# Output projection by token group, with row sums beside its last group, early operands for the second feed-forward product, and its context rows last

## The chip, the cores and the metric

The kernel runs on one core of a Trainium2 chip. TensorE (PE) multiplies matrices and accumulates in PSUM; VectorE (DVE), ScalarE (ACT) and GpSimd (POOL) work elementwise; SyncE (SP) issues DMA transfers, and so do ACT and POOL, each from a queue of its own that it works off in order. The metric is the device time of one execution in microseconds (us), the median over several runs.

## The reference

One layer of a hybrid backbone is applied to 1024 latent and 256 context tokens of width 1024. The part that the change touches begins after the three branches have been merged:

```python
x = x + gt1 * (merged @ w_out)
u2 = rmsnorm(x, g_norm2) * (1 + sc2) + sh2
x = x + gt2 * (jnp.square(jax.nn.relu(u2 @ w_ff1)) @ w_ff2)
...
y_prompt = rmsnorm(xc, g_final)
y_sample = rmsnorm(xs, g_final)
```

`w_out` is 1024 x 1024, `w_ff1` 1024 x 4096, `w_ff2` 4096 x 1024. Latent and context tokens use the same weights and different modulation vectors. Before this part stand an input norm, the combined input projection, and the pooling, gating and mLSTM branches; the change leaves them alone.

## The kernel before

**Precision.** Every large product runs on float32 operands split into a high part `hi` (rounded to float32r, an ACT cast) and a rest `lo` (a DVE subtraction), and takes three matmuls: hi by hi, hi by lo, lo by hi. So each operand that a product needs costs one ACT and one DVE instruction first.

**Tokens.** There are ten tiles of 128 tokens in three groups: 0 (tiles 0 to 3), 1 (tiles 4 to 7) and 2 (tiles 8 and 9, the context). The buffer `z` holds ten rows of 1024 floats; `xt[i]` is row i, and `zs(j)` is the j-th half row, so `xt[i]` is `zs(2i)` and `zs(2i+1)`.

**Output projection (lines 847 to 867).** The outer loop runs over four quarters q of 256 output columns. Each quarter loads two halves of `w_out` (`load_w`, lines 90 to 96: a 512 KB transfer, an ACT cast, a DVE subtraction), then goes over all ten tiles with 24 matmuls each. DVE multiplies the result by the gate and adds it to `xt`, ACT squares it for the norm. In the last quarter each tile is stored to `scr_x`, and after tiles 3, 7 and 9 `modulate_ff(g)` (lines 807 to 845) turns a finished group into the operands of the feed-forward part: a row scale whose power POOL computes (line 131), scaled rows `xn`, PE transposes (line 831), an ACT evacuation with scale and bias (lines 835 and 840), and splits on DVE (lines 836, 837, 843, 844). `load_w` has two raw and three hi and lo slots (pool `wp`), the small temporaries five (pool `tp`).

**First product (lines 876 to 1030).** Latent tokens use a 2 x 2 block scheme with seven products instead of eight: blocks B11, B21, B12, B22 of the activations (row halves by token groups 0 and 1) and four combinations T1 to T4 of them, made by 16 DVE subtractions (line 879) and split at lines 880 to 887. The 4096 hidden columns are 16 pairs fp. A `Pair` loads its two weight rows to `z`; `begin` computes the products with B11 and B21 and, between them, the four context products (`context`, lines 936 to 942); `rest` computes the other five (T4, T2, T3, T1, B22); `sums` stores the squared results to `scr_h`, `scr_c` and their combinations to `scr_s` and `scr_c`, all from ACT's queue (lines 995 to 1006). `second_sums` loads `w_ff2` rows to `zs(8..11)`, combines them on POOL (line 1015) and stores them to `scr_t`. Pool `q1`, which holds the split operands (`ring`, nine tiles, tag w), the temporaries (tag s, six) and six tiles of tag th, lies over the memory of `tp` and `wp`; it opens after the projection.

**Second product (lines 1042 to 1149).** Seven passes i = 1, 2, 6, 7, 4, 5, 3 go over the 16 pairs. `operand` loads and splits a right block (512 columns of `w_ff2` or of `scr_t`), a left block (512 columns of `scr_h` or `scr_s`, four token tiles) and a context block (128 columns of `scr_c`); 15 matmuls per pair follow, into five PSUM banks, of eight. The last pass goes twice over the pairs, with three banks and then two. `evict` combines the passes with two accumulators U and W, gates and adds them to `xt`, and `finish_rows` does the final norm and stores `y_out`. The rows `xt` are read back from `scr_x` by ten POOL transfers ahead of the passes (line 1043).

**Order.** In this part nothing is pinned: a list scheduler orders the instructions of each engine at build time, by program order as priority and by a simulated timeline.

Of the kernel before, what the change touches and what calls it, by code (L numbers as in the profile page):

```python
# [14 lines left out]
P = 128  # L15
# [34 lines left out]
def hybrid_step(  # L50
# [14 lines left out]
    sp = pa.enter_context(tc.tile_pool(name="sp", bufs=60))  # L65
    tp = pw.enter_context(tc.tile_pool(name="tp", bufs=NTMP))
    wp = pw.enter_context(tc.tile_pool(name="wp", bufs=NRAW))
# [779 lines left out]
    for q in range(4):  # L847
        wq = [load_w(w_out[q, hf], f"wo{q}_{hf}") for hf in range(2)]
        for i in range(NT):
            g, o = (i * P) // 512, (i * P) % 512  # L850
            ps = ps_mm(f"po{q}_{i}")
            for k in range(KT):
                whi, wlo = wq[k // 4]
                s = slice((k % 4) * 256, (k % 4 + 1) * 256)
                mh, ml = mT[k][g]
                PE.matmul(ps[:, :256], mh[:, o : o + P], whi[:, s], start=k == 0, stop=False)  # L856
                PE.matmul(ps[:, :256], ml[:, o : o + P], whi[:, s], start=False, stop=False)
                PE.matmul(ps[:, :256], mh[:, o : o + P], wlo[:, s], start=False, stop=k == KT - 1)  # L858
            gt = gt1[(2 if g == 2 else 0) + q // 2][:, (q % 2) * 256 : (q % 2) * 256 + 256]
            V.tensor_tensor(ps[:, :256], ps[:, :256], gt, ALU.mult)  # L860
            xq = xt[i][:, q * 256 : (q + 1) * 256]
            V.tensor_tensor(xq, xq, ps[:, :256], ALU.add)  # L862
            A.activation(ps[:, 256:512], xq, AF.Square, accum_out=fsq[:, i, q : q + 1])  # L863
            if q == 3:
                SP.dma_start(scr_x[i], xt[i])
            if q == 3 and i in (3, 7, 9):
                modulate_ff(g)
# [8 lines left out]
    for kk in range(4):  # L876
        b11, b21, b12, b22 = raw2[0][kk], raw2[0][kk + 4], raw2[1][kk], raw2[1][kk + 4]
        for out, x, y in ((b11, b12, b11), (b12, b22, b12), (b22, b22, b11), (b21, b22, b21)):
            V.tensor_tensor(out, x, y, ALU.subtract)
        for nm, t in (("T1", b11), ("T2", b22), ("T3", b12), ("T4", b21)):  # L880
            if nm == "T4" and kk != 2:
                hi, lo = (q1.tile([P, 512], F32R, tag="th", name=f"t4{i}{kk}", bufs=6) for i in "hl")
            else:
                hi, lo = slot(f"{nm}h{kk}"), slot(f"{nm}l{kk}")
            A.copy(hi, t)
            V.tensor_tensor(lo, t, hi.bitcast(F32), ALU.subtract)
            u2s[nm, kk] = hi, lo

    NFP = NFF // 2
    scr_h = [dp.tile([P, 4, 512], F32, name=f"scr_h{fp}") for fp in range(NFP)]  # L890
    scr_c = [dp.tile([2, P, 4, P], F32, name=f"scr_c{fp}") for fp in range(NFP)]
# [24 lines left out]
    class Pair:  # L916
        def __init__(self, fp):
            self.fp = fp
            self.a1, self.a2, self.b1, self.b2 = (zs(12 + 4 * (fp % 2) + i) for i in range(4))
# [24 lines left out]
        def begin(self):  # L944
            fp = self.fp
            a11, a12, a21, a22 = self.raw
            self.pc = ps_mm(f"fc{fp}")
            w = split(a11, f"a11_{fp}")
            ps = self.prod(w, "B11")
            A.copy(self.a1, ps)  # L950
            A.copy(self.a2, ps)
            self.context(0, w, 0, True)
            w = split(a12, f"a12_{fp}")
            ps = self.prod(w, "B21")
            V.tensor_tensor(self.a1, self.a1, ps, ALU.add)  # L955
            self.squared_relu(self.a1)
            self.context(0, w, 1, False)
# [31 lines left out]
        def sums(self):  # L989
# [8 lines left out]
            A.dma_start(scr_c[fp][0], self.hc.rearrange("p (q c) -> p q c", c=P))  # L998
# [5 lines left out]
            A.dma_start(scr_c[fp][1], sc.rearrange("p (q c) -> p q c", c=P))  # L1004
            for i, t in enumerate((x1, x2, a2_, x4)):
                A.dma_start(scr_s[fp][:, i, :], t)

    def second_sums(fp):

        q = [zs(8 + i) for i in range(4)]  # L1010
        for r in range(2):
            SP.dma_start(zs(8 + 2 * r, 2), w_ff2[2 * fp + r])
        b11, b12, b21, b22 = q
        for out, x, y in ((b11, b12, b11), (b12, b22, b12), (b22, b22, b11), (b21, b22, b21)):
            G.tensor_tensor(out, x, y, ALU.subtract)  # L1015
        G.dma_start(scr_t[fp], zs(8, 4).rearrange("p (q c) -> p q c", c=512))

    pairs = {}
    for fp in (0, 1):
        pairs[fp] = Pair(fp)  # L1020
    for fp in (0, 1):
        pairs[fp].begin()
    for fp in range(NFP):
        pr = pairs.pop(fp, None)
        if pr is None:
            pr = Pair(fp)
            pr.begin()
        pr.rest()
# [13 lines left out]
    for i in range(NT):  # L1042
        G.dma_start(xt[i], scr_x[i])  # L1043
# [18 lines left out]
    def operand(src, w, tag, name, early=False):  # L1062

        def room(nm, tg, dt, bufs):
            if early or tg == "l":
                return ring(nm, dt)[:, :w]
            return q2.tile([P, P if w == P else 512], dt, tag=tg, name=nm, bufs=bufs)[:, :w]

        raw = room(f"{name}r", f"{tag}r" if w == P else "raw", F32, 4)
        SP.dma_start(raw, src)  # L1070
        hi, lo = (room(f"{name}{i}", tag if tag == "l" else f"{tag}{i}", F32R, NFP if tag == "r" else 3) for i in "hl")
        A.copy(hi, raw)  # L1072
        V.tensor_tensor(lo, raw, hi.bitcast(F32), ALU.subtract)  # L1073
        return hi, lo

# [6 lines left out]
    def finish_rows(tok, final):  # L1082
        x = xt[tok]
        sq = small([P, 2], f"sq_y{tok}")
        for hf in (0, 1):
            A.activation(tmp2(f"junk_y{tok}{hf}"), x[:, hf * 512 : hf * 512 + 512], AF.Square, accum_out=sq[:, hf : hf + 1])
        s1 = small([P, 1], f"s1_y{tok}")
        V.tensor_tensor(s1, sq[:, 0:1], sq[:, 1:2], ALU.add)  # L1088
        r = rstd_of(s1, 1, f"f{tok}")
        for hf in range(2):  # L1090
            s = slice(hf * 512, hf * 512 + 512)
            V.scalar_tensor_tensor(x[:, s], x[:, s], r[:, 0:1], gf[hf], ALU.mult, ALU.mult)
            if final:
                SP.dma_start(y_out[tok][:, s], x[:, s])
        if not final:
            SP.dma_start(y_out[tok], x)

    def evict(i, j, ps):
# [3 lines left out]
        elif i == 2:  # L1102
            t = tmp2(f"c11_{j}")
            V.tensor_tensor(t, U, ps, ALU.add)
            gated_add(t, R1[j], 0)
        elif i == 6:
# [3 lines left out]
        elif i == 4:  # L1110
            t = tmp2(f"c21_{j}")
            V.tensor_tensor(t, W, ps, ALU.subtract)
            gated_add(t, R2[j], 0)
        elif i == 5:
# [3 lines left out]
            finish_rows(R2[j], False)  # L1118
        else:
            V.tensor_tensor(U, U, ps, ALU.add)  # L1120
            gated_add(U, R1[j], 1)
            finish_rows(R1[j], j == 4)

    for n_, i in enumerate((1, 2, 6, 7, 4, 5, 3)):
        scr, at, part, cols_ = PRODUCTS[i]
        rt = [None] * NFP
        for js in ((0, 1, 2), (3, 4)) if i == 3 else ((0, 1, 2, 3, 4),):
            banks = {j: p2.tile([P, 512], F32, tag="b", name=f"w{i}_{j}", bufs=8) for j in js}
            lc = None
            for fp in range(NFP):  # L1130
                early = n_ == 0 and fp < 2
                nm = f"{i}_{fp}"
                if rt[fp] is None:
                    src = scr_t[fp][:, cols_, :] if isinstance(cols_, int) else w_ff2[2 * fp + cols_[0], :, cols_[1] * 512 : cols_[1] * 512 + 512]
                    rt[fp] = operand(src, 512, "r", f"r{nm}", early)
                rh, rl = rt[fp]
                full = [j for j in js if j < 4]
                c0, c1 = full[0] * P, full[-1] * P + P
                lh, ll = operand(scr[fp][:, at, c0:c1], c1 - c0, "l", f"l{nm}_{c0}", early)
                pieces = [(j, lh[:, j * P - c0 : j * P - c0 + P], ll[:, j * P - c0 : j * P - c0 + P]) for j in full]  # L1140
                if 4 in js:
                    ch, cl = operand(scr_c[fp][part, :, at, :], P, "lc", f"lc{nm}")
                    pieces.append((4, ch, cl))
                for j, h_, l_ in pieces:
                    PE.matmul(banks[j], h_, rh, start=fp == 0, stop=False)  # L1145
                    PE.matmul(banks[j], l_, rh, start=False, stop=False)  # L1146
                    PE.matmul(banks[j], h_, rl, start=False, stop=fp == NFP - 1)  # L1147
            for j in js:
                evict(i, j, banks[j])

# [101 lines left out]
```

## Time and profile before

| | us |
|---|---|
| median of 3 runs | 2044.52 (2043.96 to 2046.18) |
| the profiled execution | 2038.69 |
| its span, first to last instruction | 2036.9 |

The profile shows one execution, and all durations below are its own; it is 5.8 us faster than the median of the runs. Its 40 slices of 51 us say, in tenths, how busy each engine was, and what clock TensorE was granted:

```profile
PE   6999999998999999999999969999999989999996
DVE  7684444449544344444444389776766555655676
ACT  6534455653111111111132265554555444434443
POOL 3000001027012122122200034334200100000000
PEclk9999999999999999999999979999999999999999
```

Counted from 0, the output projection runs in slices 21 to 23, the first feed-forward product up to slice 31, and the second one from there to the end. A group row of the profile reads: line, engine, operation, output<-inputs, shapes, count | busy us in all, mean ns of one | idle us of the engine before them, and who ended it. In the timeline the first two columns are start and duration.

### The profile page before, as it was taken

To read this page: it belongs to the slowest core of one execution; us is meant where nothing else is said; L and a number is where in the kernel's file an instruction comes from. 1 tells how busy PE (TensorE), PEld (TensorE's weight loads), DVE (VectorE), ACT (ScalarE), POOL (GpSimd) and SP (SyncE) were. 2 spreads that over 40 slices of the span, in tenths; PEclk is the share of its full clock that TensorE was granted. 3 is DMA by queue.
4 is the path that set the end of the run, shared out by engine and by line. 5 is a ranking of instruction groups with operands and counts; after the bars stand their busy time and mean duration, and the time that the engine had idled before them with its cause. 6 is when DMAs were issued, how large, how long until landed. Compare 5 with 4: busy or idle time off the path is not lost.

```text
span 2036.9 us, 28713 instructions
## 1 busy us (share of the span) xinstructions
PE 1952.8 (96%) x10688; PEld 1681.1 (83%) x10688; DVE 1168.6 (57%) x2076; ACT 776.4 (38%) x1694; POOL 322.5 (16%) x282
## 2 busy tenths in 40 slices
PE   6999999998999999999999969999999989999996
PEld 3788889996888888888889958888888878888875
DVE  7684444449544344444444389776766555655676
ACT  6534455653111111111132265554555444434443
POOL 3000001027012122122200034334200100000000
PEclk9999999999999999999999979999999999999999
DMA  8011111113222252252232146777643576555554
GB/s 322 21 34 48 51 54 42 51 58 129 94 73 83 73 184 65 63 186 73 83 99 99 44 174 230 269 265 269 232 140 135 184 257 184 176 174 174 171 170 145
DMA packets 133100, 273.93 MB, mean 134 GB/s; under 512 B 15456, under 2 KB 39904, under 8 KB 130912
## 3 DMA queue, kind: packets, MB, share of 16 engines
q1 hardware_dynamic: 97696, 193.36, 29.5%
q10 hardware_dynamic: 28224, 48.78, 6.4%
q0 software_dynamic: 7040, 29.96, 4.0%
q8 instruction: 84, 1.38, 0.3%
q14 instruction: 56, 0.46, 0.1%
HBM read 195.98 MB, written 76.06 MB: 134 GB/s over the span
## 4 chain that ended last, share of the span: by engine, by line
PE 88%; DVE 5%; DMA 3%; issue 2%; ACT 1%; POOL 1%; SPq 0%; ACTq 0%; DVEq 0%; POOLq 0%
PE w L1145 6%; PE w L1146 6%; PE w L1147 6%; PE br L124 5%; PE br L125 5%; PE br L126 5%; PE pb L759 3%; PE pb L760 3%; PE pb L761 3%; PE fT L913 3%; PE fT L912 3%; PE fT L914 3%; PE fB L914 2%; PE fB L912 2%; PE fB L913 2%; PE po L856 2%
## 5 line engine op out<-in xcount | busy, mean ns | idle before, releaser
L754 ACT ACTIVATE sg<-br 128x512 f32<-128x512 f32 (+1 forms) x72 | 37.9, 526 | 309.9 <-PE br L126 296.9
L1015 POOL TENSOR_TENSOR z<-z 128x512 f32<-128x512 f32 x64 | 97.2, 1519 | 145.3 <-DMA z<-in_w_ff 142.2
L1073 DVE TENSOR_TENSOR l_0l<-l_0r,l_0h 128x512 fp32r<-128x512 f32 (+1 forms) x112 | 75.0, 670 | 77.1 <-PE w L1146 65.5
L446 POOL PARTITION_ALL_REDUCE acc<-acc x16 | 54.2, 3431 | 327.7 <-DVE acc L439 293.9
L439 DVE SCALAR_TENSOR_TENSOR acc<-wb,scond,acc 128x512 f32<-128x512 f32 x112 | 82.3, 792 | 14.6 <-DMA wb<-in_w_ada 14.6
L768 DVE TENSOR_TENSOR sg<-pb,sg 128x512 f32<-128x512 f32 (+1 forms) x48 | 28.8, 599 | 104.9 <-PE pb L761 99.8
L131 POOL TENSOR_TENSOR rs_f<-rs_f,neghalf 128x1 f32<-128x1 f32 (+2 forms) x13 | 10.0, 772 | 489.5 <-DVE s_y L1088 357.4
L1072 ACT CAST l_0h<-l_0r 128x512 fp32r<-128x512 f32 (+1 forms) x112 | 67.4, 602 | 31.5 <-DMA l_0r<-scr_s 11.8
L933 ACT ACTIVATE z<-z 128x512 f32<-128x512 f32 x64 | 40.4, 632 | 87.4 <-DVE z L955 20.8
L766 DVE TENSOR_TENSOR z<-pb,sg 128x512 f32<-128x512 f32 (+1 forms) x24 | 14.4, 600 | 79.5 <-PE pb L761 79.5
L95 DVE TENSOR_TENSOR lo_br<-raw_br,hi_br 128x1024 fp32r<-128x1024 f32 x24 | 37.3, 1554 | 27.9 <-ACT hi_br L94 27.9
L860 DVE TENSOR_TENSOR po<-po,gt 128x256 f32<-128x256 f32 x40 | 17.3, 432 | 57.6 <-PE po L858 54.8
L94 ACT CAST hi_br<-raw_br 128x1024 fp32r<-128x1024 f32 x24 | 25.2, 1050 | 65.5 <-DMA raw_br<-in_w_in 35.9
L970 DVE TENSOR_TENSOR z<-z 128x512 f32<-128x512 f32 x64 | 48.1, 751 | 1.0
L863 ACT ACTIVATE po<-z 128x256 f32<-128x256 f32 x40 | 15.5, 387 | 78.6 <-DVE z L862 60.5
L131 POOL TENSOR_TENSOR rs_h<-rs_h,neghalf 128x4 f32<-128x4 f32 (+1 forms) x12 | 11.9, 992 | 206.4 <-DVE rs_h L130 206.3
L583 DVE SCALAR_TENSOR_TENSOR yc<-th,ccol,z 128x512 f32<-128x512 f32 (+1 forms) x12 | 7.9, 661 | 57.3 <-PE th L581 57.3
L934 ACT ACTIVATE z<-z 128x512 f32<-128x512 f32 x64 | 40.4, 631 | 1.0
L94 ACT CAST hi_wb<-raw_wb 128x1024 fp32r<-128x1024 f32 x12 | 12.6, 1048 | 63.7 <-PE br L125 44.0
L666 POOL TENSOR_TENSOR z<-z 128x1024 f32<-128x1024 f32 (+13 forms) x20 | 35.4, 1781 | 3.0 <-ACT z L651 3.0
L769 DVE TENSOR_TENSOR z<-z,sg 128x512 f32<-128x512 f32 (+1 forms) x48 | 34.5, 718 | 1.2
L1043 POOL DMA_DIRECT2D z<-scr_x x10 | 5.3, 532 | 183.8 <-ACT s_14h L903 137.8
(3409 smaller groups left out, 7146.1 us busy)
## 6 DMA issues: line engine op xcount, KB each, us to landing
z<-in_w_ff SPq DMA_DIRECT2D x64, 512.0 KB, 5.3
wb<-in_w_ada SPq DMA_DIRECT2D x32, 512.0 KB, 3.8
scr_t<-z POOLq DMA_DIRECT2D x16, 1024.0 KB, 4.2
raw_br<-in_w_in SPq DMA_DIRECT2D x24, 512.0 KB, 3.5
scr_h<-z ACTq DMA_DIRECT2D x48, 256.0 KB, 2.6
scr_s<-x ACTq DMA_DIRECT2D x48, 256.0 KB, 3.4
l_0r<-scr_h SPq DMA_DIRECT2D x48, 256.0 KB, 3.3
l_0r<-scr_s SPq DMA_DIRECT2D x48, 256.0 KB, 3.1
```

The source lines that it names most:

```text
L124: PE.matmul(ps[:, :n], whi[:, s], ahi, start=k == 0, stop=False)
L125: PE.matmul(ps[:, :n], whi[:, s], alo, start=False, stop=False)
L126: PE.matmul(ps[:, :n], wlo[:, s], ahi, start=False, stop=k == KT - 1)
L439: V.scalar_tensor_tensor(acc[j], wa[:, k2, :], scond[:, k, j : j + 1], acc[j], ALU.mult, ALU.add)
L912: PE.matmul(ps, whi[:, s], ahi, start=first and k == ks[0], stop=False)
L913: PE.matmul(ps, whi[:, s], alo, start=False, stop=False)
L914: PE.matmul(ps, wlo[:, s], ahi, start=False, stop=end and k == ks[-1])
L1015: G.tensor_tensor(out, x, y, ALU.subtract)
L1073: V.tensor_tensor(lo, raw, hi.bitcast(F32), ALU.subtract)
L1145: PE.matmul(banks[j], h_, rh, start=fp == 0, stop=False)
L1146: PE.matmul(banks[j], l_, rh, start=False, stop=False)
L1147: PE.matmul(banks[j], h_, rl, start=False, stop=fp == NFP - 1)
```

## The change

1. **Projection by group.** `project_out(g)` runs the four quarters for one token group and then `modulate_ff(g)`. `w_out` is loaded and split once per group.
2. **Row sums.** The 16 subtractions and the split of T4 stand in program order before group 2's projection. T3, T2 and T1 are split after both first pairs have begun; three of T2's four splits use the th tiles, all else slots of the main pool.
3. **Context products apart.** `begin` does B11 and B21 alone; a new method `contexts` does the four context products.
4. **Places and queues.** The pools `wp` and `tp` change places. An odd pair's results move from `zs(16..19)` to `zs(8..11)`, the weight sums from `zs(8..11)` to `zs(16..19)`. The stores of the combinations (one to `scr_c`, four to `scr_s`) go from ACT's queue to POOL's. `scr_c` holds four pairs in one 512-column row.
5. **Second product.** In the first pass the raw operands of the first ten pairs land in free half rows of `z` (`FREE`), and the splits of the first pairs in th and ring tiles. The reload of `xt` moves behind the first pass. Context blocks are loaded and split for four pairs at a time (`left_context`), and their matmuls follow the fourth pair; in the last pass they follow the evictions of the four latent banks, and the last pass goes once over the pairs.
6. **Endings.** The square and the weighting of a row's first half move to the evictions of passes 2 and 4 (`first_half`). Pass 5 also gates and adds U, so that the last pass adds its own part alone. ACT scales the first half of a finished row, DVE the second, with a store each.

```diff
-    for q in range(4):
-        wq = [load_w(w_out[q, hf], f"wo{q}_{hf}") for hf in range(2)]
-        for i in range(NT):
...
+    def project_out(g):
+        t0, n = GROUPS[g]
+        for q in range(4):
+            wq = [load_w(w_out[q, hf], f"wo{g}{q}_{hf}") for hf in range(2)]
+            for i in range(t0 // P, (t0 + n) // P):
...
+        modulate_ff(g)
...
+    def split_sum(nm):
+        g, o = ROWS_OF[nm]
+        for kk in range(4):
+            if nm == "T2" and kk < 3:
+                hi, lo = (q1.tile([P, 512], F32R, tag="th", name=f"t2{i}{kk}", bufs=6) for i in "hl")
+            else:
+                hi, lo = slot(f"{nm}h{kk}"), slot(f"{nm}l{kk}")
...
+    project_out(0)
+    project_out(1)
+    row_sums()
+    split_sum("T4")
+    project_out(2)
...
-            A.dma_start(scr_c[fp][1], sc.rearrange("p (q c) -> p q c", c=P))
+            G.dma_start(scr_c[1][fp // 4][:, :, at], sc.rearrange("p (q c) -> p q c", c=P))
             for i, t in enumerate((x1, x2, a2_, x4)):
-                A.dma_start(scr_s[fp][:, i, :], t)
+                G.dma_start(scr_s[fp][:, i, :], t)
...
     for fp in (0, 1):
         pairs[fp] = Pair(fp)
+        pairs[fp].begin()
+    for nm in ("T3", "T2", "T1"):
+        split_sum(nm)
     for fp in (0, 1):
-        pairs[fp].begin()
+        pairs[fp].contexts()
...
+    FREE = (0, 2, 16, 18, 12, 14, 4, 6, 8, 10)
...
+    def right(src, i, fp):
+        if n_ == 0 and fp < len(FREE):
+            raw = zs(FREE[fp])
...
+    def left(src, i, fp):
+        raw = zs(FREE[fp] + 1) if n_ == 0 and fp < len(FREE) else ring(f"l{i}_{fp}r", F32)
...
+            for j in range(4):
+                times(j, fp, l_, j * P)
+            if fp % 4 == 3 and i != 3:
+                context_rows(fp // 4)
+        if i == 3:
+            for j in range(4):
                 evict(i, j, banks[j])
+            for j in range(NFP // 4):
+                context_rows(j)
...
+        evict(i, 4, banks[4])
+        if n_ == 0:
+            for k in range(NT):
+                G.dma_start(xt[k], scr_x[k])
```

More of the change, by code (lines that the diff above doesn't have):

```diff
@@ L1027, in hybrid_step @@
             pr.begin()
+            pr.contexts()
         pr.rest()
@@ L1060, in hybrid_step, with split2 @@
     }
[L1062 to L1071, printed above, removed]
+    FREE = (0, 2, 16, 18, 12, 14, 4, 6, 8, 10)
+    def split2(raw, room):
+        hi, lo = room("h"), room("l")
         A.copy(hi, raw)
@@ L1105, in evict @@
             gated_add(t, R1[j], 0)
+            first_half(R1[j])
         elif i == 6:
@@ L1124, in hybrid_step @@
     for n_, i in enumerate((1, 2, 6, 7, 4, 5, 3)):
         scr, at, part, cols_ = PRODUCTS[i]
[L1126 to L1148, printed above, removed]
-                evict(i, j, banks[j])
```

172 lines of the change are left out of this document (106 added, 66 removed).

## The prediction

> **What bounds the kernel now.** I read the page's first part, then busy time by stretch, then what TensorE (PE) waited for, then the order of time around each hole. The first row shows the bound: PE is busy 96% of the span, so the change can only win where PE stands still or runs at a reduced clock.
>
> ```profile
> PE 1952.8 (96%) x10688; PEld 1681.1 (83%) x10688; DVE 1168.6 (57%) x2076; ACT 776.4 (38%) x1694; POOL 322.5 (16%) x282
> ```
>
> The stretches I cut show where that is; the columns are length, then busy time (and instructions) of PE, weight loads, DVE, ACT and POOL, then granted clock, DMA share and GB/s.
>
> ```profile
> 1074.00:1190.00 116.00, 116.00 (x972) 115.90 (x971) 50.72 (x115) 34.07 (x101) 2.97 (x4) 1.00 0.26 98
> 1190.00:1226.00 36.00, 15.71 (x64) 10.84 (x64) 33.51 (x64) 20.63 (x42) 14.82 (x11) 0.62 0.38 136
> 1226.00:1262.00 36.00, 36.00 (x205) 31.63 (x204) 31.91 (x44) 21.76 (x43) 15.21 (x10) 1.00 0.55 198
> 1410.00:1420.00 10.00, 7.25 (x37) 6.61 (x37) 3.37 (x7) 5.17 (x11) 4.34 (x4) 0.83 0.55 218
> 1625.00:1641.00 16.00, 8.53 (x26) 5.62 (x26) 8.87 (x17) 7.46 (x16) 1.38 (x3) 0.83 0.95 332
> 1979.00:1992.00 13.00, 7.19 (x30) 4.98 (x29) 10.14 (x20) 4.32 (x10) 2.15 (x3) 1.00 0.91 319
> 2023.80:2036.90 13.10, 0.00 (x0) 0.00 (x0) 5.40 (x12) 2.06 (x6) 1.08 (x2) 0.66 0.20 80
> ```
>
> Five holes: **A** after the output projection (1190 to 1226), **E** inside the first feed-forward product, **B** at the start of the second product, **C** at the start of its last one, **D** the tail. In A, PE idles 36.00 - 15.71 = 20.3 us, and a mean clock of 0.62 means that about three quarters of the stretch ran at half clock, so half of 15.71 x 3/4, 5.9, is lost to the clock too: 26 us. B: 7.5 idle, and 0.83 of 16 us costs half of the work done in its slow third, 2: 9.5. C: 5.8. What ends the holes:
>
> ```profile
> PE pt L831 <- ACT xn L823: 8.9, 2, 8.5
> PE pt L831 <- DVE u20c L837: 7.0, 1, 7.0
> PE w L1145 <- ACT l_0h L1072: 6.4, 2, 5.5
> PE fc L912 <- ACT hc L941: 2.8, 1, 2.8
> ACT l_0h L1072 <- DMA l_0r<-scr_s: 9.0, 6, 3.1
> ```
>
> A is DVE's: 33.51 of 36 us busy, while PE waits for the transposes of the context group and finds little else, because `begin` (lines 944 to 960) mixes the first products with context operands (line 952), and those come last.
>
> **Term A: projection by group, row sums beside its last group.** PE's work stays. First and last of 960 projection matmuls (40 tiles x 24):
>
> ```profile
> 1071.10 0.28 PE L856 MATMUL po<-hi_wo,m0h 128*128 128x256 f32 x1
> ...
> 1189.65 0.28 PE L858 MATMUL po<-lo_wo,m7c 128*128 128x256 f32 x1
> ```
>
> 118.6 us / 960 = 0.12 us a matmul, so 16 tiles take 47 us (groups 0 and 1 each) and 8 tiles 24 (group 2). w_out is loaded and split three times instead of once. The prices:
>
> ```profile
> L94 ACT CAST hi_wo<-raw_wo 128x1024 fp32r<-128x1024 f32 x8 | 8.2, 1042 | 5.5 <-PE br L125 4.9 <-PE po L857 0.5
> L95 DVE TENSOR_TENSOR lo_wo<-raw_wo,hi_wo 128x1024 fp32r<-128x1024 f32 x8 | 9.7, 1220 | 7.1 <-ACT hi_wo L94 5.5 <-PE po L858 1.6
> L860 DVE TENSOR_TENSOR po<-po,gt 128x256 f32<-128x256 f32 x40 | 17.3, 432 | 57.6 <-PE po L858 54.8 <-DMA gt<-scr_mod 2.7
> L862 DVE TENSOR_TENSOR z<-z,po 128x256 f32<-128x256 f32 x40 | 16.8, 419 | 1.1
> L879 DVE TENSOR_TENSOR u2r<-u2r,u2r 128x512 f32<-128x512 f32 x16 | 11.0, 718 | 0.7 <-ACT u2r L840 0.7
> L825 DVE TENSOR_SCALAR xn<-z,rs_f 128x256 f32<-128x256 f32 x20 | 9.1, 506 | 2.2 <-POOL rs_f L131 1.8
> L844 DVE TENSOR_TENSOR u2l<-u2r,u2h 128x512 fp32r<-128x512 f32 x12 | 8.2, 685 | 0.1
> L843 DVE CAST u2h<-u2r 128x512 fp32r<-128x512 f32 x12 | 5.1, 421 | 0.7 <-ACT u2r L840 0.7
> L840 ACT ACTIVATE u2r<-pt,sh,a 128x512 f32<-128x512 f32 x16 | 11.5, 767 | 0.0
> raw_wo<-in_w_out SPq DMA_DIRECT2D x8, 512.0 KB, 4.1
> ```
>
> 16 more loads: 16 x 1.042 = 16.7 us of ACT, 16 x 1.220 = 19.5 of DVE, and 16 transfers of 512 KB on SP's queue (4.1 us each, DMA share there 0.26: hidden; past SP go also the scr_x stores, now in three batches). Beside projection group 1 DVE has 8 splits (9.8), 16 evictions of 0.85 (13.6), and group 0's modulation, 8 x 0.506 + 8 x (0.421 + 0.685) = 12.9: 36 of 47 us, hidden. Beside group 2 it has 9.8 + 8 x 0.85 (6.8) + group 1's modulation, 4.0 + 4 x 1.106 = 8.5, + 16 row sums (11.5) + the four T4 splits (2.7): 39 of 24 us. ACT there has 8 casts (8.3), 8 of L840 (6.1), the other 8 row scalings (some 4) and four T4 casts (2.5): 21 of 24 before the squares. That is not hidden. Next PE can run B11 and B21 of both pairs, which need no context operand:
>
> ```profile
> 1242.25 0.40 PE L912 MATMUL fT<-t4h,a_0h 128*128 128x512 f32 x1
> 1242.48 0.40 PE L913 MATMUL fT<-t4l,a_0h 128*128 128x512 f32 x1
> ```
>
> 0.23 us apart, 48 of them, 11 us. They cover the context group's chain (today 8.5 us of wait at its head), which also stops queueing on POOL behind a weight sum: the new scratch lies in xt[8] and xt[9], free only after that chain has read them. DVE meanwhile: 4 x 0.506 and 16 casts and subtractions of 256 columns at L862's 0.42 (8.7), 4 splits at L844's 0.685 (2.7), 2 additions (1.4). Then contexts, 96 matmuls of 0.12, 11.5 us, beside 4 splits and the 12 of T3, T2, T1 (10.9). From the start of group 2's projection PE has 24 + 11 + 11.5 = 46 us, DVE 39 + 12.8 + 11 = 63. Neighbouring records overlap by about a tenth, so 57: DVE is 11 us short. Bounds of what is left of A: 5 (five us of T splits are due only later) and 22 (the 17 without overlap, and 5 of handshakes). I take 13.5: the 11, and 2.5 for the first ring tiles, which wait for the projection's last matmuls, and their split. **Gain 12.5.**
>
> POOL's sums can worsen this; the two rows are the sum and a split that met one:
>
> ```profile
> 1235.95 1.78 DVE L886 TENSOR_TENSOR T4l<-u2r,T4h 128x512 fp32r<-128x512 f32 x1
> L1015 POOL TENSOR_TENSOR z<-z 128x512 f32<-128x512 f32 x64 | 97.2, 1519 | 145.3 <-DMA z<-in_w_ff 142.2
> ```
>
> 1.1 us more than a free 0.68. The Trainium skill (SBUF — State Buffer, Who interferes with whom) says that a DVE instruction with two SBUF inputs and a GpSimd one that reads SBUF exclude each other for a whole instruction; the trace agrees with its 1.78. By that rule eight sums of two pairs would each hold back one split, 8.8 us, and the time would be 2026; I leave it out of the sum since four of the T splits and all row sums move ahead of POOL's first sum.
>
> **Term E.** ACT issues nine stores per pair (lines 995 to 1006) and stands in order behind them:
>
> ```profile
> 1411.12 0.33 ACTq L1006 DMA_DIRECT2D scr_s<-z  x1
> 1411.98 0.63 ACT L933 ACTIVATE z<-z 128x512 f32<-128x512 f32 x1 [3.65 <-DMA scr_s<-x]
> 1412.93 0.38 PE L912 MATMUL fc<-u20c,a_7h 128*128 128x256 f32 x1 [2.75 <-ACT hc L941]
> ```
>
> Five of the nine, those of the sums, go to POOL's queue. Queued behind them there are `second_sums`' subtractions and their store, which the second product's third pass reads first, over 100 us after its start, and the next pair's. Gain 2.8 idle and about 1 of clock: **3.5** (0 to 4). The Trainium skill (TensorE: Matmul & The Clock Gate, HAM oscillation) puts the idle gap that halves the clock at some 3.4 us; here 2.75 already left 0.83 over 10 us, so the measurement decides. By the page alone E would be 2.8 and the time 2018.
>
> The hc stores and the sc stores get four 512 B pieces a row where a contiguous 2 KB row was written; reads get one where four were. The first reader of a late one (pair 15's) is product 1's last context block, 40 us on: I take zero (bounds: 2 us lost, 2 gained, a landing either way).
>
> **Term B: first operands in the row buffer.** Product 1's raws for ten pairs go into z as its slots fall free, and the reload of ten rows (512 KB each) leaves the transition, where DMA is at 0.95 and
>
> ```profile
> 1630.93 0.32 SPq L1070 DMA_DIRECT2D l_0r<-scr_h  x1
> 1637.23 0.62 ACT L1072 CAST l_0h<-l_0r 128x512 fp32r<-128x512 f32 x1 [3.50 <-DMA scr_s<-x]
> ```
>
> takes 6.3 us from issue to use. Slots 0 to 3 fall free with pair 14, the th tiles after pair 15's T2, which 36 matmuls (8 us) follow; three splits of 0.62 and 0.69 fit. 2 us stay: **gain 7.5** (0 to 9.5).
>
> **Term C.** Product 5's evictions grow. Today per tile two sums, two for the gate and two scalings:
>
> ```profile
> L1115 DVE TENSOR_TENSOR accU<-accU,w 128x512 f32<-128x512 f32 x5 | 3.4, 680 | 0.0
> L1092 DVE SCALAR_TENSOR_TENSOR z<-z,rs_f,gf 128x512 f32<-128x512 f32 x20 | 14.1, 748 | 2.9 <-POOL rs_f L131 2.9
> ```
>
> 4 x 0.68 + 2 x 0.75 = 4.2; after, 6 x 0.68 + 0.75 = 4.8, so 3 us more in five tiles. Against it the last product has four banks per pair, 2.72 us of PE per two splits instead of 2.04. y_out still stands ahead of loads on SP. **Gain 2** (-4 to 5).
>
> **Term D.** Context rows last: 48 matmuls x 0.227 = 10.9 us cover four banks' endings (per bank DVE 3 x 0.7, 8.4, with 4 splits 11.2), and one bank's ending is left instead of two.
>
> ```profile
> 2023.99 0.68 DVE L1120 TENSOR_TENSOR accU<-accU,w 128x512 f32<-128x512 f32 x1
> 2029.30 1.41 DVE L1092 SCALAR_TENSOR_TENSOR z<-z,rs_f,gf 128x512 f32<-128x512 f32 x2 [0.72 <-POOL rs_f L131]
> ```
>
> From the last matmul (2023.8) to the last result are 6.9 us, for two endings that queue on DVE; less the other bank's three sums at the gate (2.0) and half a scaling row (0.7), 4 are left. Half-row scaling moved to products 2 and 4 hides in stretches where DVE idles. Gain 3, less 1 for the crowded DVE: **2** (0 to 3).
>
> **Sum:** 12.5 + 3.5 + 7.5 + 2 + 2 = 27.5. The profiled execution took 2038.69 (span 2036.9 and 1.8 around it), 5.8 below the median 2044.52; it would take 2011, the median **2017**.
>
> **Rivals.**
> 1. Everything closes: bounds 21 + 4 + 9.5 + 4 + 3 = 41: 2003. For it: DVE idles 65 us beside the projection today. Against: DVE's 39 in 24. Chance 0.12.
> 2. DVE starves PE in projection group 2: row sums are written ahead of it, so its splits and evictions wait, and A keeps 23 of 26. 2027. For: 39 in 24; three hi/lo slots hold one and a half quarters. Against: sums become ready only one by one. 0.15.
> 3. The operands aren't early: z slots or th tiles fall free only with pair 15, B gains nothing: 2025. For: one tensor z holds everything. Against: pair 14's slots and the weight sums' are not touched by pair 15. 0.05.
> 4. Rivals 2 and 3 together, with C at -4: 27.5 - 9.5 - 7.5 - 6 = 4.5, within the bound of no change, 2040. 0.06.
> 5. Slower: at each quarter's border the second half's split waits for the slot that the old quarter's last tile frees: 1.04 + 1.22 us. PE covers 2.9 with two half tiles. There are 12 quarters instead of 4; if DVE's queue delays each of the 8 new borders by 2.7 us beyond the cover, with 1.4 of clock as in E, 33 us go: +5, 2050. It decides from 27.5/8 = 3.4 us a border. For: group 2. Against: in groups 0 and 1 DVE has 11 us to spare. 0.07.
>
> My forecast (2010 to 2023) has 0.55. Range 2005 to 2034: it leaves out 4, 5 and the far end of 1. A measurement of this kernel can tell 0.2%, 4 us, from no change: faster 0.87, same 0.06, slower 0.07.
>
> **What would show it.** Right: B11 of pair 1 before the first context product; idle PE below 15 us between projection and rest; no PE wait on l_0h at product 1's start; hc waits gone; one bank after the last matmul. Wrong: DVE waits of po matmuls on lo_wo in group 2 over 8 us; POOL's queue delaying weight sums until scr_t is read; a PE gap over 3 us at product 3.

## The result, and the profile after

The changed kernel takes 2061.56 us (median of 4 runs, 2058.84 to 2063.38), against 2044.93 (2043.96 to 2046.18) for the kernel before, measured beside it: a ratio of 1.008, with an interval from 1.0062 to 1.0097. The forecast was 2017; it is 17 us slower instead. The profiled execution took 2058.84, its span is 2057.1.

The page of the changed kernel, the busy times and, of the slices (51 us each), the rows of PE and its clock:

```profile
PE 1963.4 (95%) x10688; PEld 1681.9 (82%) x10688; DVE 1179.0 (57%) x1997; ACT 788.2 (38%) x1620; POOL 369.6 (18%) x362
...
PE   6999999998999999999999979999999999989995
...
PEclk9999999999999999999999989999999999999998
```

The dip in slice 23 (hole A) is still there but shallower. Slice 32 (hole B) now reads 9, while slice 35 reads 8 and the last one 5, where the kernel before has 9 and 6. A slice that reads 9 hides up to 10% of idle time, though, and much of the loss sits there. Cut into stretches (length, then busy time and instructions of PE, weight loads, DVE, ACT, POOL, then granted clock, DMA share, GB/s) the changed kernel shows it:

```profile
1190.00:1226.00 36.00, 25.57 (x132) 21.10 (x131) 34.75 (x67) 23.47 (x49) 7.83 (x7) 0.81 0.29 116
1410.00:1420.00 10.00, 10.00 (x57) 8.75 (x56) 9.09 (x12) 5.15 (x9) 7.58 (x8) 1.00 0.73 289
1610.00:1680.00 70.00, 64.91 (x279) 51.53 (x279) 37.70 (x59) 35.21 (x63) 8.44 (x16) 1.00 0.83 284
1680.00:1800.00 120.00, 120.00 (x531) 99.19 (x529) 63.10 (x106) 46.11 (x85) 0.00 (x0) 1.00 0.57 176
1800.00:1940.00 140.00, 124.04 (x505) 94.55 (x505) 63.56 (x108) 46.10 (x88) 0.00 (x0) 0.99 0.45 135
1980.00:2000.00 20.00, 15.53 (x58) 12.66 (x59) 18.39 (x36) 8.47 (x19) 6.21 (x5) 0.83 0.35 108
2022.00:2046.00 24.00, 13.24 (x52) 10.23 (x51) 11.40 (x20) 7.71 (x16) 3.31 (x4) 0.79 0.40 132
```

The first three rows are the holes that the forecast spoke of: A idles 10.4 us (36.00 - 25.57) where it idled 20.3, E is gone, and the start of the second product idles 5.1 of 70 us, where the kernel before idles 7.5. The same two stretches of the second product in the kernel before:

```profile
1610.00:1680.00 70.00, 62.53 (x273) 50.44 (x272) 33.89 (x63) 28.63 (x60) 5.32 (x10) 0.95 0.76 252
1800.00:1940.00 140.00, 140.00 (x620) 115.95 (x619) 79.66 (x146) 56.15 (x126) 0.00 (x0) 1.00 0.57 174
```

Passes 2 and 6 (1680 to 1800) are full. Between 1800 and 1940, in the passes 7, 4 and 5 of the second product, PE now idles 16 us, where it idled none, and gets through 505 matmuls instead of 620, while no engine and no transfer is near its limit (DVE 63.56 of 140, DMA 0.45): such a stretch waits for latency, not for throughput. At the start of the last pass, where the kernel before has hole C, 4.5 us are idle (and the clock is down to 0.83), and near its end 10.8, which are new. What PE waited for in the second half of the changed kernel, in us, times and the longest:

```profile
PE w L1189 <- ACT c_0h L1090: 12.7, 2, 10.8
PE w L1190 <- DVE l_3l L1091: 5.9, 2, 4.7
PE w L1189 <- ACT l_11h L1090: 2.5, 2, 1.5
...
PE w L1189 <- DVE accW L1162: 2.1, 1, 2.1
```

So two kinds of operand are late: left blocks (`l_`), a little and often, and once a context block (`c_0`).

**Left blocks: one tile goes round.** The order of time around 1825, for all engines but PE (start, duration, in brackets the idle time before and its releaser):

```profile
1823.48 0.62 ACT L1090 CAST l_12h<-l_12r 128x512 fp32r<-128x512 f32 x1 [4.59 <-PE w L1191]
1824.13 0.69 DVE L1091 TENSOR_TENSOR l_12l<-l_12r,l_12h 128x512 fp32r<-128x512 f32 x1 [4.04 <-ACT l_12h L1090]
1824.85 0.32 SPq L1112 DMA_DIRECT2D l_13r<-scr_s  x1
1827.99 0.62 ACT L1090 CAST l_13h<-l_13r 128x512 fp32r<-128x512 f32 x1 [3.89 <-DMA l_13r<-scr_s]
1828.64 0.69 DVE L1091 TENSOR_TENSOR l_13l<-l_13r,l_13h 128x512 fp32r<-128x512 f32 x1 [3.82 <-ACT l_13h L1090]
1829.36 0.32 SPq L1112 DMA_DIRECT2D l_14r<-scr_s  x1
```

Block 13's load is issued the moment block 12's subtraction ends, block 14's the moment block 13's ends: 1824.85 to 1829.36, 4.5 us a block, made of 3.1 from issue to cast, 0.6 and 0.7. PE needs 2.72 us for the 12 matmuls of a block. A load that waits for the previous split is one that lands in the tile which that split has just read. The built program says so too. Its nine ring tiles, numbered 0 to 8, are given to the left blocks as follows, three digits for the raw, the hi and the lo tile of blocks 0 to 15:

```
pass 2: 476 385 201 432 674 581 602 536 475 182 406 134 571 285 602 436
pass 7: 142 871 508 635 624 617 680 536 542 571 508 635 624 617 680 536
pass 4: 542 571 508 635 624 617 680 536 542 571 508 635 624 617 680 536
```

In pass 2, raw blocks next to each other get different tiles, and the stretch 1680 to 1800 with passes 2 and 6 is full. From block 3 of pass 7 four raws in a row get tile 6, then four get tile 5, and so on through pass 4: the hi and lo tiles of four blocks hold all eight others, so one tile is left for landing. The kernel before never gets there, because from the third pair on its left raws land in the four `raw` tiles that the right blocks use too (`operand`, tag "raw"), and only hi and lo lie in the ring. In `left`, the change sends the raw to the ring as well.

**Context block: behind the results.** SP's queue in the last pass of the changed kernel:

```profile
2028.83 0.33 SPq L1146 DMA_DIRECT2D out_y<-z  x1
2029.26 0.38 SPq L1148 DMA_DIRECT2D out_y<-z  x1
2029.69 0.46 SPq L1123 DMA_DIRECT2D c_0r<-scr_c  x1
```

The last matmul of the latent banks starts at 2023.05. The context blocks that PE needs then are loaded from 2029.69 on, behind the stores of two rows (the second is shown) that must first be evicted, normed and scaled. PE goes on at 2034.20: of its 10.8 us some 6.3 pass before the load is issued, and 4.5 are load and cast.

### The profile page after: what moved, and what is told of

It reads as the page before. It is cut to its first block, busy times and chain, and to the rows that moved or that the text cites. A ratio compares the mean times of both kernels' runs of the same rounds, so it can differ in the third digit from the quotient of the medians.

```text
span 2057.1 us, 28426 instructions
## 1 busy us (share of the span) xinstructions
PE 1963.4 (95%) x10688; PEld 1681.9 (82%) x10688; DVE 1179.0 (57%) x1997; ACT 788.2 (38%) x1620; POOL 369.6 (18%) x362
## 4 chain that ended last, share of the span: by engine, by line
PE 64%; DMA 12%; issue 9%; DVE 6%; POOL 6%; ACT 2%; SPq 0%; POOLq 0%; ACTq 0%; DVEq 0%
PE br L124 5%; PE br L125 5%; PE br L126 5%; PE w L1190 4%; PE w L1189 4%; PE w L1191 4%; POOL z L1036 3%; DMA z<-in_w_ff 3%; DMA scr_t<-z 3%; PE pb L759 3%; PE pb L760 3%; PE pb L761 3%; PE po L860 1%; PE po L858 1%; PE po L859 1%
## 5 line engine op out<-in xcount | busy, mean ns | idle before, releaser
L1144 POOL TENSOR_TENSOR rs_y<-rs_y,neghalf 128x1 f32<-128x1 f32 x10 | 10.1, 1011 | 395.9 <-DVE rs_y L1143 395.9
L990 DVE TENSOR_TENSOR z<-z 128x512 f32<-128x512 f32 x64 | 53.4, 838 | 1.0
L1027 POOL DMA_DIRECT2D scr_s<-x x48 | 26.3, 549 | 61.4 <-DVE x L1021 53.6
L95 DVE TENSOR_TENSOR lo_wo<-raw_wo,hi_wo 128x1024 fp32r<-128x1024 f32 x24 | 29.2, 1220 | 13.0 <-ACT hi_wo L94 12.9
L865 ACT ACTIVATE po<-z 128x256 f32<-128x256 f32 x40 | 15.5, 387 | 53.7 <-DVE z L864 47.1
L666 POOL TENSOR_TENSOR z<-z 128x1024 f32<-128x1024 f32 (+13 forms) x20 | 35.4, 1782 | 3.0 <-ACT z L651 3.0
L447 POOL TENSOR_TENSOR acc<-acc,bt 1x512 f32<-1x512 f32 x16 | 20.2, 1277 | 57.9 <-issue 57.9
```

The source lines that it names most:

```text
L95: eng.tensor_tensor(lo, raw, hi.bitcast(F32), ALU.subtract)
```

## The experiments

They ran in three series, each beside the kernel before, whose median was 2046.74, 2044.62 and 2044.33. What is compared below with 2018.89 (first series) or with 2012.82 (second series) is mostly of a later series, and such a difference is uncertain by some 2 us from that alone.

### Left raws in tiles of their own; context loads ahead; both

The six `th` tiles are idle from the second pass on. The first edit puts the left raws there:

```diff
-        raw = zs(FREE[fp] + 1) if n_ == 0 and fp < len(FREE) else ring(f"l{i}_{fp}r", F32)
+        raw = (zs(FREE[fp] + 1) if n_ == 0 and fp < len(FREE) else ring(f"l{i}_{fp}r", F32) if n_ == 0
+               else q1.tile([P, 512], F32, tag="th", name=f"l{i}_{fp}r", bufs=6))
```

> Only edit to the changed kernel: from the second pass of the second product on, the raw left blocks land in the six th tiles, which are idle there, and no longer in the nine ring tiles that also hold the split left blocks. Ring theory: in passes 7, 4 and 5 (1800 to 1940 us) the ring is full of split blocks and only one of its nine tiles serves as the landing place, so a left block takes load 3.1 + cast 0.62 + subtraction 0.69 = 4.5 us where its 12 matmuls take 2.72 us; with places of their own the 16 us that TensorE idles between 1800 and 1940 go, and most of what it idles on l_ blocks after 1960, so the time falls by 14 to 20 us, to 2042 to 2048. Rival, too little cover: 12 matmuls per block (2.72 us) cannot cover the latency of a load whatever the place, so the idle time stays and the time is within 4 us of 2061.6. Rival, evictions: TensorE waits because the vector engine is busy with evictions, which this edit leaves; within 4 us of 2061.6.

Measured: **2027.45** us (ratio to the kernel before 0.991, 0.989 to 0.993), 34 less than the changed kernel and twice what was expected. The same stretch as above, of this kernel:

```profile
1800.00:1940.00 140.00, 140.00 (x620) 115.95 (x619) 76.40 (x122) 57.38 (x101) 0.00 (x0) 1.00 0.56 165
```

Not one us of idle time is left, with 12 matmuls a block: 2.72 us are cover enough, and both rivals fall. The gain is more than the 16 us of idle time because idle time is not all that the loop cost: in this stretch PE now gets through 620 matmuls instead of 505, and 115 matmuls at 0.227 are 26 us (the 505 also took 0.246 us of busy time each, the 620 only 0.226). Another 7 went between 1980 and 2000, where 58 matmuls stood in a stretch that holds 88 and the wait for l_3l is gone. What stays is the wait for c_0h, 10.2 us here.

The second edit, alone, loads three of four context blocks before the evictions:

```diff
         if i == 3:
+            lcs = [left_context(part, at, i, j) for j in range(3)]
             for j in range(4):
                 evict(i, j, banks[j])
             for j in range(NFP // 4):
-                context_rows(j)
+                context_rows(j, lcs[j] if j < 3 else None)
```

> Only edit to the changed kernel: in the last pass three of the four context blocks are loaded and split in program order before the evictions of the four latent banks, and their matmuls still stand behind these evictions. Queue theory: TensorE waits 10.8 us for c_0h because the context loads stand on SyncE's queue behind the y_out stores of the rows just finished; with the loads ahead of those, the wait falls below 1 us and with the clock lost in it the time falls by 10 to 13 us, to 2049 to 2052. Rival, engines: the splits themselves queue on ScalarE and VectorE behind the four endings (8 to 11 us), so the wait stays above 5 us and the gain is below 5 us.

Measured: **2060.48** (1.0071, 1.005 to 1.0091), a gain of 1, within the noise, where 10 to 13 were expected. The waits of this kernel name the block that is late now:

```profile
PE w L1189 <- ACT c_3h L1090: 6.6, 1, 6.6
...
PE w L1189 <- ACT c_0h L1090: 2.3, 1, 2.3
```

and its SP queue shows why:

```profile
2034.34 0.33 SPq L1146 DMA_DIRECT2D out_y<-z  x1
2034.77 0.38 SPq L1148 DMA_DIRECT2D out_y<-z  x1
2035.20 0.45 SPq L1123 DMA_DIRECT2D c_3r<-scr_c  x1
```

The fourth load has taken the place of the first behind the stores: 6.6 + 2.3 us of waiting where 10.8 were, and part of these 1.9 us was given back in the passes before, which idle 17.0 us here between 1800 and 1940 instead of 16.0. By itself the run decides little: it had moved three of four blocks only.

> Both edits together: raw left blocks in the th tiles from the second pass on, and three context blocks of the last pass loaded before the evictions. If ring and queue are two separate losses, the gains add up: 2061.6 - 17 - 11.5 = 2033, 2028 to 2039, below the kernel before. If one loss only takes the place of the other (the vector engine is late by itself), 2045 or more.

Measured: **2018.89** (0.9874, 0.9853 to 0.9896). Beside the first edit, the same context edit that gained 1 alone gains 8.6, and the wait for c_3h is down to 2.7. One more step puts the fourth block ahead too (`range(4)`, and four instead of three hi and lo tiles):

> The mended kernel (left raws in the th tiles, context blocks of the last pass ahead of its evictions) with all four context blocks ahead instead of three, in four hi and lo tiles instead of three. Queue theory: in the mended kernel c_3r is issued at 2001.71 behind two y_out stores, TensorE waits 2.7 us for c_3h, and half of the last twelve matmuls run at a reduced clock; with the fourth load ahead too, the wait goes and the time falls by 3 to 5 us from 2018.9, to 2014 to 2016. Rival: the last matmuls then only wait for the endings of the latent banks on VectorE, so that the end stays: 2018 to 2020.

Measured: **2012.82** (0.9832, 0.9814 to 0.9849), 6.1 less. This kernel beats both; from 1980 to its last matmul PE has no idle time:

```profile
1980.00:2001.00 21.00, 21.00 (x93) 17.09 (x91) 9.81 (x18) 5.47 (x12) 3.31 (x4) 1.00 0.23 86
```

From 2061.56 to 2012.82 are 48.7 us: 34.1 for the tiles, 14.6 for the queue, taken in this order. The two are not independent: with three context blocks ahead first, the queue gives 1.1 and the tiles then 41.6 (2060.48 to 2018.89).

### The parts that were to gain

The second product of the kernel before, with everything else as changed (only its reads of `scr_c` follow the new layout):

> The changed kernel with parts 5 and 6 undone: the second feed-forward product and the endings are those of the kernel before (context blocks per pair, raw operands not in the row buffer, two runs of the last pass, both halves scaled at the end), only its reads of scr_c follow the new layout. My theory: the projection by group, the row sums and the stores on GpSimd's queue are worth what they showed (TensorE idles 10.4 us instead of 20.3 between 1190 and 1226, clock 0.81 instead of 0.62, no idle time near 1410), and all of the loss is in parts 5 and 6: 2044.9 - 10 - 3 - 3.5 = 2028, 2024 to 2032. Rival, shared memory traffic: the stores in 512-byte pieces and the stores from GpSimd also slow the reads of the second product, which then loses time here as well: above 2038.

Measured: **2026.21** (0.991, 0.9885 to 0.9934), 20.5 less than the runs of the kernel before beside it (2046.74). The interval allows 13 to 23. All of the loss is in parts 5 and 6: as written they cost 35.4 us (2061.56 less 2026.21), and with both mends they gain 13.4. The rival with its 2038 falls; what the 512-byte pieces cost by themselves no run sets apart.

Three runs take a part away from the kernel with three contexts ahead (2018.89). The stores of the combinations back on ACT's queue (`G.dma_start` to `A.dma_start`, two lines):

> The mended kernel with the stores of the combinations (one to scr_c, four to scr_s per pair) issued from ScalarE's queue again, as in the kernel before. Term E of the prediction: ScalarE stands in order behind these stores and TensorE waits for hc once, 2.8 us and about 1 us of clock: 3.5 us more, 2022 to 2023. Rival: the hole near 1410 came from when pair 7's sums met other work, and with the new order of pairs the stores cost nothing: within 1.5 us of 2018.9. Rival: POOL's queue delays weight sums, so ScalarE's queue is better: 2015 to 2017.

Measured: **2026.58** (0.9903, 0.9887 to 0.9919), 7.7 slower; by the ratios of the two series it is 5.9, and their intervals just overlap. In the first product PE idles 4.5 us (384.00 - 379.54), where the kernel with the stores on POOL idles 0.3:

```profile
1226.00:1610.00 384.00, 379.54 (x2016) 327.93 (x2015) 277.82 (x417) 187.17 (x354) 97.02 (x76) 1.00 0.64 221
```

```profile
PE fT L928 <- ACT s_8h L919: 2.0, 1, 2.0
PE fc L928 <- ACT hc L957: 1.9, 2, 0.9
```

The waits are on ACT, as the theory says, but in more places than one. Next, row sums and T4's split behind group 2's projection:

```diff
-    row_sums()
-    split_sum("T4")
     project_out(2)
+    row_sums()
+    split_sum("T4")
```

> The mended kernel with the 16 row sums and the split of T4 in program order behind group 2's projection instead of ahead of it. Theory of the prediction: these 14 us of VectorE are better spent beside the projection; behind it they push the splits of T3, T2 and T1 back and TensorE waits for them: 4 to 10 us slower than 2018.9. Rival, from the trace: the evictions of group 2's last tile and its row scale stand behind row sums and T4 splits on VectorE (1198.8 to 1204.2 us), so TensorE waits 8.2 us for xn; with the sums behind, this wait falls by 3 to 5 us and B11 and B21 cover the sums: 2014 to 2017. If the two balance: within 2 us.

Measured: **2015.99** (0.9857, 0.9834 to 0.988), 2.9 faster; but the runs reach from 2014.0 to 2022.2, and the same edit on the faster kernel takes that back:

> The changed kernel with every edit that helped: left raws apart, four context blocks ahead in the last pass, row sums and T4's split behind group 2's projection. If the gains add: 2012.8 less 3, 2008 to 2012. If the gain of the row sums was only a shift of the last pass's order: 2012 to 2015.

Measured: **2013.05** (0.9848, 0.9834 to 0.9861), against 2012.82 without it. Against that kernel, hole A gets 2 us shorter (27.13 instead of 25.06 us busy of 36) and the first product loses 1 (382.82 instead of 384.00 of 384).

Where the row sums stand is worth nothing that these runs can tell. The third, the two context products of `begin` back between and behind B11 and B21:

> The mended kernel with part 3 undone for the first half of each pair: the two context products with a11 and a12 stand between B11 and B21 and behind it again, as in the kernel before (T3, T2 and T1 are split after that). Theory of the prediction: contexts apart let B11 and B21 of both pairs cover the context group's chain, 11 us of TensorE; with the contexts inside, that cover is lost where the chain is late: 3 to 8 us slower than 2018.9. Rival, from the trace: the transposes of the context group are issued ahead of B11 on TensorE anyway, and ScalarE casts a_0h only behind the chain, so no cover exists and nothing changes: within 1.5 us.

Measured: **2020.87** (0.9877, 0.9858 to 0.9896), 2.0 slower, within what two such series differ by. Hole A is as deep (25.77 busy of 36), but one wait for hc, 2.7 us, is back in the first product.

Two runs take a part away from the best kernel (2012.82). The context rows of the last pass behind every fourth pair (`if fp % 4 == 3` without `and i != 3`):

> The kernel with three mends (left raws apart, four context blocks ahead) with the context rows of the last pass behind every fourth pair, as in the other passes, so that all five banks are evicted behind the last matmul. If context rows last cover four endings as the prediction's term D has it, four endings of 2.1 us of VectorE (two at 0.69, one at 0.75) move behind the last matmul: 6 to 9 us slower than 2012.8. Rival: without a burst of context work the last pass runs without a wait and the endings overlap on three engines: within 3 us of 2012.8.

Measured: **2019.21** (0.9878, 0.9864 to 0.9891), 6.4 slower, as the theory has it. Both kernels end their matmuls at the same time (2002.0 and 2001.0), but this one then takes 15.5 us for five endings, the other 10.1 for one. And the early operands undone, `xt` reloaded ahead of the passes:

> The same base with the early operands undone: no raw block of the first pass lands in the row buffer, none is split into th or ring tiles of its own choice, and the ten rows of xt are reloaded ahead of the passes, as in the kernel before. Term B of the prediction: 7.5 us slower than 2012.8, about 2020. Rival, from the trace: the base still idles 5.3 us between 1640 and 1680, for left blocks 10 to 14, which have no place in the row buffer and queue behind it, so the hole has moved and the term is worth 2 to 4 us: 2015 to 2017.

Measured: **2030.18** (0.9921, 0.9907 to 0.9934), 17.4 slower, far outside either theory. The start of the second product, first without the early operands, then with them:

```profile
1610.00:1680.00 70.00, 57.72 (x208) 42.19 (x207) 35.28 (x54) 32.19 (x55) 5.27 (x10) 0.88 0.84 286
```

```profile
1610.00:1680.00 70.00, 64.68 (x280) 51.84 (x279) 41.34 (x64) 38.30 (x67) 9.63 (x18) 1.00 0.91 319
```

It idles 12.3 us instead of 5.3, at a mean clock of 0.88, worse than the kernel before (62.53, 0.95). The loss is all in the first pass: from the last matmul of the first product to the first one of the second pass are 77 us here (1613.9 to 1690.7), 59 with the early operands (1612.6 to 1671.9) and 65 in the kernel before (1625.1 to 1690.4). But the edit does not restore the old first pass. The splits of the first pairs keep their th and ring tiles, and the raw left blocks of this pass land in the ring, as later ones do in the changed kernel, and not in the `raw` tiles, where the kernel before puts them from the third pair on. So the 17.4 us are not the price of the places in `z` alone; how much of them is the ring was not tried.

### The raws in the ring, in the kernel before

```diff
-        raw = room(f"{name}r", f"{tag}r" if w == P else "raw", F32, 4)
+        raw = ring(f"{name}r", F32)[:, :w] if tag == "l" else room(f"{name}r", f"{tag}r" if w == P else "raw", F32, 4)
```

> The kernel before with one edit alone: raw left blocks land in the ring (nine tiles, shared with the split ones), as in the changed kernel, instead of in the four raw tiles. If the shared ring by itself starves TensorE: 4.5 us per left block against 3.4 of its 15 matmuls, over some fifty blocks, 20 to 50 us slower than 2044.6. If it takes the one-tile loop, it depends on which tile each block was given: here consecutive raw blocks get different tiles in all passes, so several loads are under way at once, and the time stays within 6 us of 2044.6.

Measured: **2061.29** (1.008, 1.0066 to 1.0094), 17 slower. Neither side had this. The loop theory is right for the steady passes, in which neighbouring raws have different tiles:

```profile
1610.00:1680.00 70.00, 59.15 (x258) 46.42 (x258) 38.21 (x74) 32.47 (x70) 6.37 (x12) 0.95 0.83 277
1740.00:1980.00 240.00, 240.00 (x1060) 198.75 (x1059) 133.66 (x257) 97.95 (x214) 0.00 (x0) 1.00 0.58 169
1980.00:2042.00 62.00, 53.33 (x214) 40.06 (x213) 40.22 (x100) 23.12 (x72) 5.29 (x8) 0.97 0.40 130
```

240 us without an idle one. But the shared ring also has a price where many blocks are wanted at once: 10.9 us idle at the start of the second product (before: 7.5), 8.7 in the last pass (before: 5.8). One wait in the first product is also twice as long, 5.7 us instead of 2.8. In the built programs the order on every engine is the same up to the end of the first product, so this is a difference between two executions, not the edit's:

```profile
PE fc L912 <- ACT hc L941: 5.7, 1, 5.7
```

That the sum is again 17 is chance, since the time goes in other places than in the changed kernel. In the profiles this kernel is 19.8 us longer than the kernel before: 5 up to the end of the first product, where the programs are alike, 7 in the first pass, and most of the rest in the last one.

## Why the prediction was wrong

**The step that failed** is the reading of part 5: it has no term for where the left blocks land. I read the second product by its matmuls, splits and evictions and priced places in `z` for the first pass (term B), the evictions (C) and the tail (D). That `left` puts every raw block of the six later passes into the ring, where the kernel before used the `raw` tiles, is one expression in the diff and has no row in the trace of before. In the edit that gives these blocks tiles of their own it is 34 us. Term C did speak of cover, but for the last pass and in the wrong currency: "four banks per pair, 2.72 us of PE per two splits instead of 2.04" counts what the engines must do, and the loop of load, cast and subtraction (4.5 us a block) binds while the engines are idle more than half of the time.

**Term D assumed what term C had written down.** "Context rows last: 48 matmuls x 0.227 = 10.9 us cover four banks' endings" needs the operands of these matmuls to be there. C's last sentence has "y_out still stands ahead of loads on SP", and this is just what made c_0 late by 10.8 us: the endings that the matmuls were to cover stood ahead of the matmuls' own loads. With the loads ahead, the term is right, and without context rows last the same kernel is 6.4 slower. The tail after the last matmul is 10.1 us against 13.1, the 3 of its upper bound.

**Term A** (12.5): right in size, partly wrong in its reason. Parts 1 to 4 alone gain 20.5, of which the stores are some 6 to 8 (by the run that put them back), so some 13 are left; the trace has 9.9 us less idle time and a clock of 0.81 instead of 0.62. Of the left 10.4 us, 8.2 are one wait, and it is not the splits that come late. In the changed kernel:

```profile
1204.38 1.71 ACT L823 ACTIVATE xn<-z,rs_f 128x256 f32<-128x256 f32 x4 [0.24 <-POOL rs_f L131]
...
1204.94 2.40 PE L831 MATMUL pt<-cst,xn 128*128 128x128 f32 x10 [8.21 <-ACT xn L823]
...
1210.38 0.61 ACT L919 CAST a_0h<-z 128x512 fp32r<-128x512 f32 x1
...
1211.04 0.79 PE L928 MATMUL fB<-u2h,a_0h 128*128 128x512 f32 x1 [1.16 <-ACT a_0h L919]
...
1212.06 0.41 PE L928 MATMUL fc<-u20c,a_0h 128*128 128x256 f32 x1
```

B11 and B21 were to cover the context group's chain. They do not: PE has the transposes ahead of them, and ACT casts a_0h only behind the chain. Nor do they stand apart: the first context matmul (`fc`) runs 1 us after the first one of B11, since nothing pins the order. So the first of the signs that were to show the prediction right, B11 of pair 1 before the first context product, did not come. This fits with parts 2 and 3, moved singly, changing little. What is left to have gained is the order of the projection by groups, which puts group 0's and group 1's modulation beside matmuls; this is concluded from the rest, as no run changes the order alone.

**Term E** (3.5, bounds 0 to 4): right mechanism, and more than its bounds, 7.7 or 5.9, though the noise between the two series leaves the 3.5 just possible. I priced the one hole that the trace of before showed, and it was 5.7 instead of 2.8 us long in another execution of the same order (the last experiment); without the move the new order has waits on ACT at several pairs.

**Term B** (7.5): near. Against the kernel before, the hole shrank from 7.5 idle to 5.3 in the best kernel, and the clock came back; by the time from the first product's last matmul to the second pass it is 6 (65 to 59), of which the kernel with the old second product has 2 already (63, from 1612.3 to 1675.3). What is left are blocks 10 to 14, which have no place in `z`. The run without early operands, 17.4 slower, does not price the term, for it also puts the raw left blocks of the first pass into the ring.

**Term C** (2): in the best kernel the 5.8 us at the start of the last pass are gone, the upper end of its bounds. No run prices the 512-byte pieces alone.

**Signs and rivals.** Of the other signs for the prediction all came (A idles 10.4, below 15; no wait on l_0h at the start; the hc waits gone; one bank after the last matmul), and the kernel was slower all the same. The last of the signs against it came as well: PE gaps over 3 us in the last pass, 4.7 and 10.8. The slower one (5) named quarter borders; PE's longest wait for a `w_out` split in these kernels is under 1 us. Rivals 2 and 4 did not come either. None spoke of a ring or of a load behind stores. (Rival 1 adds term C with 4, where the term's own bound is 5; with that it is 2002, not 2003.) The terms that I had sum to 27.5, and the best kernel, in which the two mishaps are mended, gains 31.8. That these are near is in part luck, since E and C came out larger and B smaller; the list was incomplete.

## What to carry to other kernels

When a change rewrites where an operand lands, count for each shared pool of tiles what it holds before and after, and compute the round trip of a block (load, cast, subtraction) divided by the landing tiles that are surely free; compare that with PE's time per block, even if every engine is half idle. Before work is moved behind something to cover it, look up what its own operands queue behind. And look for small steady losses with stretches of 100 us or more: the page's tenths hardly show them. The 16 us between 1800 and 1940 made one 9 an 8.

## What the runs showed of the hardware

A short gap can cost more than its length. In the changed kernel:

```profile
1846.25 0.80 PE L1189 MATMUL w<-r_0h,l_0h 128*128 128x512 f32 x1 [2.10 <-DVE accW L1162]
1846.85 0.63 PE L1190 MATMUL w<-r_0h,l_0l 128*128 128x512 f32 x1
1847.28 0.63 PE L1191 MATMUL w<-r_0l,l_0h 128*128 128x512 f32 x1
...
1849.76 0.40 PE L1191 MATMUL w<-r_1l,l_1h 128*128 128x512 f32 x1
1850.00 0.39 PE L1189 MATMUL w<-r_1h,l_1h 128*128 128x512 f32 x1
```

Behind 2.10 us of idle time the matmuls come 0.43 us apart for 3.5 us, and 0.23 apart after that, so the gap costs about 1.6 us more. The gaps of about 1 us at each left block between 1800 and 1840 left the clock at 1.00. The Trainium skill (TensorE: Matmul & The Clock Gate, HAM oscillation) puts the gap that matters at some 3.4 us; here 2.10 was enough, as 2.75 was in the kernel before, and the measurement decides. But the length alone does not tell: in the run with three context blocks ahead and nothing else, PE waited 2.14 us at the same place, and the matmuls were 0.23 apart almost at once:

```profile
1848.75 0.50 PE L1189 MATMUL w<-r_0h,l_0h 128*128 128x512 f32 x1 [2.14 <-DVE accW L1162]
1849.09 0.40 PE L1190 MATMUL w<-r_0h,l_0l 128*128 128x512 f32 x1
```
